# A hybrid decoder layer on one core: three buffers in RWKV's preparation, and small products that wait for the state chain's next step

## Chip, cores and metric

The kernel runs on one core of one Trainium2 chip. The metric is the device time of one execution in microseconds (us); lower is better. Times are medians over runs.

## The reference

One layer (DEPTH 1) on x of shape 1 x 512 x 2048 in float32. The hidden size of the feed-forward part is 5632.

```python
h = rms_norm(x, attn_norm_g)
qa, ka, va, qb, kb, vb, rw = split(h @ w_in)
ya = diff_attention(qa, ka, va, ...)             # 4 heads, two softmaxes subtracted, ALiBi
yb = sliding_window_attention(qb, kb, vb, ...)   # 8 query, 2 key heads, window 128, sinks
feats = token_shift(rw, rwkv_mu)
r, k, v, wl, al, gl = split(feats)               # 16 heads of 64
decay = exp(-exp(-softplus(-(w0 + tanh(wl) @ w2)) - 0.5))
a = sigmoid(a0 + al @ a2);  g = sigmoid(gl) @ g2
kk = normalised(k * k_k);  k = k * (1 + (a - 1) * k_a)
# token by token, for every head:
S = S * w_t + (S @ a_t) b_t^T + v_t k_t^T        # a_t = -kk, b_t = kk * a
y_t = S @ r_t
yc = (group_norm(y) * ln_w + ln_b + bonus) * g
x = x + concat(ya, yb, yc) @ w_out
x = x + (silu(h2 @ w_gate) * (h2 @ w_up)) @ w_down   # h2 = rms_norm(x)
return rms_norm(x, final_norm_g)
```

## The kernel before

**Layout and dense products.** Everything is kept transposed: 128 partitions hold features, 512 columns hold tokens. Each projection onto 128 features is 16 slices of the input's 2048 features, and each slice takes three matmuls, since the float32 operands are split into a high and a low part in a reduced format (high times high, low times high, high times low): 48 "dense" products a projection, which all go through `mm` (L131). A weight is loaded by SyncE's queue (L204), rounded to its high part on ScalarE (ACT, L208) and its low part is taken on VectorE (DVE, L209). The program runs the mixers' 43 projections with a step structure (the last of the gates' inputs, then k, r and v for each of 8 pairs of RWKV heads, then the attention's), then w_out, then the feed-forward part (44 gate, 44 up, then down).

**The small work between them.** The RWKV and attention work is cut into steps, written as Python generators that stand in lanes. After each dense product, `pump` looks at all lanes, and lets each lane whose time is due emit its next step; a generator's `yield` says how much later its next step is due, in a planner's microseconds (`self.now`, which `mm` moves on), or, with nothing, when the planner takes the step's work on DVE and ACT for done. A generator that needs something unfinished yields and looks again at the next pump. TensorE executes in the order in which the products are emitted; the other engines' order is set by a scheduler that heeds priorities. Float32 products of the small steps are not split.

**One pair of RWKV heads** (512 tokens, 8 chunks of 64) goes through these generators:

- `rates` (L457-490): two products z (with w2) and pa (with a2) and from them, on ACT and DVE, the decay W, its inverse V and a.
- `prep` (L494-615): the norm kn, kk, and bk (L526, L531), two operands side by side; the transposes bt of bk in two halves of four, each copied from PSUM to bkn on ACT (L541); ar (L548, L550), holding -kk times W and r times W; zl, copied from ar on ACT (L560); the Gram products gr of bk with ar in two halves u of 4 chunks and 2 heads, in two pieces each with `yield 0.4` between; their parts are masked on DVE (L577) into linv, zl and gr, three masks for each of four PSUM tiles; linv's blocks go to DRAM (L588); then vt (v by token) with its copies to uv (L602), and bon and bv (L607, L612).
- `inverse` (L617-645), lane 1: after the blocks are read back in another layout (x), 31 steps of forward substitution on DVE (xt L637, xy L638), and the store of the result, xi, to DRAM (L642).
- `join` (L648-685), lane 7: `yield 7`, load of xi into linv (L653), `yield 6`, then three groups of 16 products 32x32: px, pt and po, which complete the inverse.
- `chain` (L688-735), lane 2: 8 chunks in order, each with products z, u and S and their copies on ACT and DVE in between, and y into a PSUM tile of its own.
- `post` (L737-765), lane 6: the variance product var, the normalisation, the gate's products g.

bt of pair p waits until the chain of pair p-2 is at its end, since bkn has two buffers; so has every one of ar, zl, gr, uv and linv.

**PSUM** is in pools: pd, two tiles for the dense products; pm, two tiles (z, pa, kn, bt, gr, vt, bon); pc, three (chain, join, post and the attention); py, one for y. A product into a tile waits until the work that read the tile's earlier content is done.

Of the kernel before, what the change touches and what calls it, by code (L numbers as in the profile page):

```python
# [14 lines left out]
P = 128  # L15
# [73 lines left out]
class Kernel:  # L89
    def __init__(self, tc, ins, out, dbg=None, stop=None):  # L90
        self.tc = tc
        self.nc = tc.nc
        self.i = ins
        self.out = out
        self.dbg = dbg or {}
        self.stop = stop
        self.lanes = [[], [], [], [], [], [], [], []]
        self.order = [self.lanes[j] for j in (2, 7, 6, 5, 0, 1, 3, 4)]
        self.done = set()
        self.flags = set()  # L100
        self.now = 0.0
        self.due = {}
        self.free = {"DVE": 0.0, "Activation": 0.0}
        self.last = 0.0
        self.slack = 0.3
        self.lead = 300
# [56 lines left out]
    def pump(self):  # L163
        moved = False
        for lane in self.order:
            if lane:
                name, gen = lane[0]
                if self.due.get(name, 0.0) > self.now:
                    continue
                moved = True  # L170
                self.last = self.now
                try:
                    wait = next(gen)
                    self.due[name] = self.now + wait if wait else self.last + self.slack
                except StopIteration:
                    lane.pop(0)
                    self.done.add(name)
                self.last = self.now
        return moved

    def need(self, name):
        for _ in range(100000):
            if name in self.done:
                return
            if not self.pump():
                self.now = min(self.due[lane[0][0]] for lane in self.order if lane)
# [192 lines left out]
    def mixer_items(self, enter):  # L379
# [35 lines left out]
        self.linv = [lp.tile([P, NCH, P], F32, name=f"linv{j}") for j in range(2)]  # L415
# [3 lines left out]
        keep = rp.tile([P, NCH, 65], F32, tag="pn", name="keep")  # L419
# [37 lines left out]
    def rates(self, hp):  # L457
        nc, rp = self.nc, self.rp
        q = self.in_flight[hp]
        while hp and f"prep{hp - 1}" not in self.done:  # L460
            yield
        if not hp:
            yield 15
        ch = slice(hp * P, (hp + 1) * P)
        w2 = rp.tile([97, P], F32, tag="w2", name=f"w2_{hp}", bufs=4)
        a2 = rp.tile([96, P], F32, tag="w2", name=f"a2_{hp}", bufs=4)
# [27 lines left out]
    def prep(self, hp):  # L494
        nc, rp = self.nc, self.rp
        q = self.in_flight[hp]
        while "k" not in q or f"rates{hp}" not in self.done:
            yield
# [34 lines left out]

        while hp >= 2 and f"loop{hp - 2}" not in self.done:
            yield
        bkn = rp.tile([P, NCH, P], F32, tag="bkn", name=f"bkn{hp}", bufs=2)
        for u in range(2):
            ps = self.pm.tile([P, 4, P], F32, tag="m", name=f"bt{hp}_{u}")
            for n in range(4):
                self.tr(ps[:, n, :], bk[:, u * 4 + n].rearrange("p a c -> p (a c)"))  # L540
            nc.scalar.copy(out=bkn[:, u * 4:u * 4 + 4, :], in_=ps)  # L541
            yield
        q["bkn"] = bkn
        while "r" not in q:
            yield
        r = q["r"]
        ar = rp.tile([P, NCH, 2, C], F32, tag="ar", name=f"ar{hp}", bufs=2)
        nc.vector.scalar_tensor_tensor(out=ar[:, :, 0, :], in0=c3(kk), scalar=-1.0, in1=W[:, :, 0:64],  # L548
                                       op0=ALU.mult, op1=ALU.mult)
        nc.vector.tensor_tensor(out=ar[:, :, 1, :], in0=c3(r), in1=W[:, :, 1:65], op=ALU.mult)  # L550

        nc.vector.tensor_tensor(out=a, in0=a, in1=r, op=ALU.mult)
# [3 lines left out]
        zl = rp.tile([P, 2, NCH, C], F32, tag="zl", name=f"zl{hp}", bufs=2)  # L556
        L = self.linv[hp % 2]
        gr = rp.tile([P, 2, NCH, C], F32, tag="gr", name=f"gr{hp}", bufs=2)
        for h in range(2):
            nc.scalar.copy(out=zl[HALF[h], h, 1:], in_=ar[HALF[h], 1:, 0, :])  # L560
        mask = self.cst("mask", P)
        for u in range(2):
# [3 lines left out]
            for j in range(4):  # L566
                n = 4 * u + j
                for h in range(2):
                    self.mm(ps[h][:, j, :], bk[HALF[h], n], ar[HALF[h], n], start=True, stop=True)
                if j == 1:  # L570
                    yield 0.4
            for h in range(2):
# [7 lines left out]
                masked(zl[ks, h, us], ks, 0)  # L580
                masked(gr[:, h, us], slice(0, P), 1)
        q.update(zl=zl, L=L, gr=gr, ar=ar)
# [8 lines left out]
        while "v" not in q:  # L591
            yield
# [12 lines left out]
        yield  # L605
        rkm = rp.tile([P, P], F32, tag="w2", name=f"rkm{hp}", bufs=4)
# [3 lines left out]
        yield  # L610
# [5 lines left out]
    def inverse(self, q):  # L616
# [7 lines left out]
        y = rp.tile([P, 8, 32], F32, tag="i1", name="xy")  # L624
# [7 lines left out]
        tmp = rp.tile([P, 8, 32], F32, tag="i3", name="xt")  # L632
# [14 lines left out]
    def join(self, q):  # L647
# [3 lines left out]
        yield 7  # L651
        for h, b, bl in blocks:
            nc.sync.dma_start(out=L[bl, :, bl], in_=d[h, b].rearrange("n i g t -> (i g) n t"))  # L653
        yield 6
# [17 lines left out]
        pt = rp.tile([P, NCH, 32], F32, tag="pt", name="pts")  # L672
# [15 lines left out]
    def chain(self, q):  # L688
        nc, rp = self.nc, self.rp
        hp, zl, L, gr, ar, uv, bkn = (q[n] for n in ("hp", "zl", "L", "gr", "ar", "uv", "bkn"))  # L690
        while hp and f"y{hp - 1}" not in self.done:
            yield
        py = self.py.tile([P, T], F32, tag="y", name=f"y{hp}")
        q["g2"] = g2 = rp.tile([P, 2, P], F32, tag="g2", name=f"g2_{hp}", bufs=2)
        nc.sync.dma_start(out=g2, in_=self.i["g2"][:, :, hp * P:(hp + 1) * P])


        for n in range(NCH):
            pz = self.pc.tile([P, C], F32, tag="c", name=f"z{hp}_{n}")
            for h in range(2):  # L700
                ks = slice(0, P) if n else HALF[1 - h]
                self.mm(pz[HALF[h]], zl[ks, h, n], uv[ks, n, h])
# [4 lines left out]
            if n:  # L707
                for h in range(2):
                    self.mm(py[HALF[h], n * C:(n + 1) * C], uv[HALF[h], n, h], ar[HALF[h], n, 1], start=True,
# [12 lines left out]
            if n < NCH - 1:  # L722
# [3 lines left out]
                with self.urgent():  # L726
                    for h in range(2):
# [4 lines left out]
                        else:  # L732
                            nc.vector.tensor_scalar(out=s, in0=pS[hs], scalar1=d, scalar2=None, op0=ALU.mult)
            for h in range(2):
                self.mm(py[HALF[h], n * C:(n + 1) * C], uv[:, n, h], gr[:, h, n], start=(n == 0), stop=True)
            yield
        self.lanes[6].append((f"chain{hp}", self.post(q, py)))  # L737

    def post(self, q, py):
# [10 lines left out]
        yield  # L750
# [4 lines left out]
        yield  # L755
        ps = self.pc.tile([P, T], F32, tag="c", name=f"g{hp}")
        for j in range(2):
            self.mm(ps, q["g2"][:, j, :], self.gl[j], start=(j == 0), stop=(j == 1))
        yield
# [61 lines left out]
    def attention_setup(self):  # L821

        nc = self.nc
        while f"inv{NPAIR - 1}" not in self.done or f"loop{NPAIR - 2}" not in self.done:
            yield
        dist = self.rp.tile([P, 768], F32, tag="ar", name="dist", bufs=2)
# [25 lines left out]
    def diff_head(self, h, q, vtag):  # L852
        nc, rp = self.nc, self.rp
        while "setup" not in self.done:
            yield
        bias = rp.tile([P, T], F32, tag="h", name=f"bias{h}", bufs=2)
        nc.scalar.mul(out=bias, in_=self.dist, mul=DIFF_SLOPES[h])
        while "k" not in q:
            yield
# [3 lines left out]
        def scores(blk):  # L863
# [5 lines left out]
            p = rp.tile([P, 2, T], F32, tag=("bk", "i1")[blk % 2], name=f"pa{h}_{blk}")  # L869
# [16 lines left out]
        def turned(blk):  # L886
# [4 lines left out]
            wt = rp.tile([P, 4, P], F32, tag=("pt", "pn")[blk % 2], name=f"wts{h}_{blk}")  # L891
# [10 lines left out]
        while "v" not in q:  # L902
            yield
        vn = self.natural(q["v"], vtag, f"van{h}")
        while f"chain{NPAIR - 1}" not in self.done:
            yield
# [23 lines left out]
    def swa_values(self, kv):  # L930
        while "v" not in kv:
            yield
# [3 lines left out]
    def swa_tile(self, i, q, kv):  # L936
# [5 lines left out]
        while "q" not in q:  # L942
            yield
# [8 lines left out]
        def scores(n):  # L952
# [5 lines left out]
            p = rp.tile([P, 2, 256], F32, tag=("bk", "i1")[n % 2], name=f"pb{i}_{n}")  # L958
# [19 lines left out]
        def turned(n):  # L978
# [5 lines left out]
            wt = rp.tile([P, 2, 2, P], F32, tag=("pt", "pn")[n % 2], name=f"wtsb{i}_{n}")  # L984
# [28 lines left out]
    def mixes(self, js):  # L1013
# [4 lines left out]
        for n, j in enumerate(js[::2]):  # L1018
            for e in range(2):
                while self.mix[j + e] is None:  # L1020
                    yield
# [269 lines left out]
```

## Time and profile before

| | |
|---|---|
| median of 3 runs | 2465.69 us (2463.95 to 2465.7) |
| the profiled execution | 2460.77 us |
| its span in the profile | 2459.0 us |
| granted TensorE clock, mean | 0.994 |
| ScalarE / VectorE / GpSimd instructions | 1391 / 2121 / 157 |

The profile is of one execution. Its span leaves out 1.8 us of the execution's own time. In a line of groups the columns are: line, engine, operation, output<-inputs, tile shape, count | busy us, mean ns of one | idle us of the engine just before and what ended it. A timeline's row has the start, the duration, and in brackets the idle time ahead of it with its releaser. A window's row has the length of the stretch, then busy time and number of instructions of each engine, then the granted clock (1.00 is full). Matmuls are pipelined, so that a row's duration is longer than its step to the next row's start. PE is TensorE, PEld its weight loads, SPq SyncE's DMA queue.

### The profile page before, as it was taken

The page shows a single profiled execution, that of the slowest core. Times are in us where ns is not written, and L with a number is a line of the kernel's source. Part 1 is how long each engine was busy: PE and PEld are TensorE (multiplying, and loading weights), DVE is VectorE, ACT ScalarE, POOL GpSimd, SP SyncE. Part 2 cuts the span into 40 slices and gives each one's busy share as a digit, 9 for nine tenths or more (in the row PEclk, how much of TensorE's full clock was granted, in tenths as well). Part 3 has the DMA queues.
Part 4 walks back from the last instruction along what each step waited for, and adds up shares of the span by engine and source line. Part 5 has one row for each costly group of instructions (what it writes and reads, how often), then busy time and mean ns, then how long its engine had stood idle before and what let it go on. Part 6 is the DMA issues. An engine that isn't in the chain of part 4 may idle for free.

```text
span 2459.0 us, 30832 instructions
## 1 busy us (share of the span) xinstructions
PE 2415.4 (98%) x12328; PEld 1915.2 (78%) x12328; DVE 1181.9 (48%) x2121; ACT 813.8 (33%) x1391; POOL 99.4 (4%) x157
## 2 busy tenths in 40 slices
PE   8999999999999999999999999999999999999997
PEld 6766666676677778888888888888888888888887
DVE  7567776675544544434343434343434333343437
ACT  5445555444434423322222122222222222222224
POOL 3000000000000003100000000000000000000006
PEclk9999999999999999999999999999999999999999
DMA  5222222222223433222322322322232232232224
GB/s 176 91 77 75 84 75 83 66 82 85 90 86 100 146 124 103 95 95 97 101 95 95 101 96 94 99 98 95 96 101 94 95 101 96 94 100 98 94 96 136
DMA packets 103793, 240.04 MB, mean 98 GB/s; under 512 B 34906, under 2 KB 43746, under 8 KB 103650
## 3 DMA queue, kind: packets, MB, share of 16 engines
q1 hardware_dynamic: 98754, 231.39, 29.4%
q10 hardware_dynamic: 4896, 6.69, 0.8%
q8 instruction: 97, 1.59, 0.3%
q14 instruction: 46, 0.38, 0.0%
HBM read 227.55 MB, written 10.49 MB: 97 GB/s over the span
## 4 chain that ended last, share of the span: by engine, by line
PE 87%; DVE 2%; ACT 1%; DMA 1%; issue 1%; SPq 0%; POOL 0%; DVEq 0%; ACTq 0%; POOLq 0%
PE pg L131 19%; PE pu L131 19%; PE pd L131 19%; PE po L131 7%; PE pd_v L131 3%; PE pd_k L131 2%; PE pd_r L131 2%; PE pd_va L131 2%; PE pd_qa L131 2%; PE pd_qb L131 2%; PE pd_ka L131 1%; PE y L131 1%; PE z L131 1%; PE S L131 1%; PE pd_kb L131 1%
## 5 line engine op out<-in xcount | busy, mean ns | idle before, releaser
L131 PE MATMUL pd<-al,wh_wd 128*128 128x512 f32 (+1 forms) x768 | 285.3, 371 | 0.6 <-DVE al L1141 0.6
L131 PE MATMUL pd<-ah,wh_wd 128*128 128x512 f32 (+1 forms) x768 | 285.5, 372 | 0.4 <-DVE y L1160 0.4
L131 PE MATMUL pd<-ah,wl_wd 128*128 128x512 f32 (+1 forms) x768 | 285.2, 371 | 0.0
L131 PE MATMUL pu<-x1h,wh_wu 128*128 128x512 f32 x704 | 274.3, 390 | 0.0
L131 PE MATMUL pu<-x1l,wh_wu 128*128 128x512 f32 x704 | 273.9, 389 | 0.0
L131 PE MATMUL pu<-x1h,wl_wu 128*128 128x512 f32 x704 | 273.9, 389 | 0.0
L131 PE MATMUL pg<-x1h,wl_wg 128*128 128x512 f32 x704 | 273.9, 389 | 0.0
L131 PE MATMUL pg<-x1l,wh_wg 128*128 128x512 f32 x704 | 273.9, 389 | 0.0
L131 PE MATMUL pg<-x1h,wh_wg 128*128 128x512 f32 x704 | 273.9, 389 | 0.0
L1160 DVE TENSOR_TENSOR y<-y,pd 128x512 f32<-128x512 f32 (+1 forms) x192 | 122.5, 641 | 207.8 <-PE pd L131 207.6
L208 ACT CAST wh_wd<-raw_wd 128x1024 fp32r<-128x1024 f32 x96 | 101.0, 1052 | 356.9 <-PE pd L131 177.2
L208 ACT CAST wh_wu<-raw_wu 128x1024 fp32r<-128x1024 f32 x88 | 92.7, 1053 | 366.7 <-PE pu L131 144.8
L208 ACT CAST wh_wg<-raw_wg 128x1024 fp32r<-128x1024 f32 x88 | 92.7, 1054 | 362.8 <-PE pg L131 144.9
L209 DVE TENSOR_TENSOR wl_wg<-raw_wg,wh_wg 128x1024 fp32r<-128x1024 f32 x88 | 107.8, 1225 | 171.4 <-ACT wh_wg L208 171.4
L209 DVE TENSOR_TENSOR wl_wu<-raw_wu,wh_wu 128x1024 fp32r<-128x1024 f32 x88 | 107.8, 1225 | 133.5 <-ACT wh_wu L208 133.5
L131 PEld LDWEIGHTS pd<-al,wh_wd 128*128 128x128 f32 x768 | 144.7, 188 | 25.7 <-DVE al L1141 0.8
L131 PEld LDWEIGHTS pd<-ah,wh_wd 128*128 128x128 f32 x768 | 144.7, 188 | 25.6 <-issue 0.5
L131 PEld LDWEIGHTS pd<-ah,wl_wd 128*128 128x128 f32 x768 | 144.7, 188 | 24.9
L131 PEld LDWEIGHTS pu<-x1h,wh_wu 128*128 128x128 f32 x704 | 132.1, 188 | 27.6 <-issue 0.2
L131 PEld LDWEIGHTS pu<-x1l,wh_wu 128*128 128x128 f32 x704 | 132.1, 188 | 27.6 <-issue 0.2
L131 PEld LDWEIGHTS pu<-x1h,wl_wu 128*128 128x128 f32 x704 | 132.1, 188 | 27.5
L131 PEld LDWEIGHTS pg<-x1h,wl_wg 128*128 128x128 f32 x704 | 132.1, 188 | 27.4
(357 smaller groups left out, 4100.4 us busy)
## 6 DMA issues: line engine op xcount, KB each, us to landing
raw_wd<-in_w_down SPq DMA_DIRECT2D x96, 512.0 KB, 3.2
raw_wg<-in_w_gate SPq DMA_DIRECT2D x88, 512.0 KB, 3.7
raw_wu<-in_w_up SPq DMA_DIRECT2D x88, 512.0 KB
raw_wo<-in_w_out SPq DMA_DIRECT2D x32, 512.0 KB, 3.5
raw_k<-in_w_in SPq DMA_DIRECT2D x16, 512.0 KB, 3.8
raw_r<-in_w_in SPq DMA_DIRECT2D x16, 512.0 KB, 4.3
raw_v<-in_w_in SPq DMA_DIRECT2D x16, 512.0 KB, 3.7
x<-in_xT SPq DMA_DIRECT2D x16, 256.0 KB, 4.9
```

Of the source, the lines that this page charges most:

```text
L131: self.tc.keep_in_program_order(self.nc.tensor.matmul(out, lhsT, rhs, start=start, stop=stop))
L208: nc.scalar.copy(out=hi[:, :kn * m], in_=s)
L209: nc.vector.tensor_tensor(out=lo[:, :kn * m], in0=s, in1=hi[:, :kn * m].bitcast(F32), op=ALU.subtract)
L1160: nc.vector.tensor_tensor(out=o, in0=o, in1=ps, op=ALU.add)
```

## The change

Four things are edited together.

**Three buffers.** `ar` and `zl` become one tile Z, three blocks of 64 columns for each chunk: blocks 0 and 1 hold, for the two heads, -kk times W in that head's partitions and the masked Gram part in the other's; block 2 holds r times W. The two copies zl<-ar a pair go; -kk times W is written in two operations of 64 partitions in place of one of 128. Z, gr and linv have three buffers each; to make room, w2/a2/rkm share three in place of four, g2 has one, and other tiles move to other tags.

**Riding.** A generator that needs something unfinished yields a condition, kept in `self.until`, and becomes due when the condition holds. Steps with products (all lanes but 1, the substitution and mixes, and 5, the token shifts) are not emitted as soon as they are due, but when the state chain's lane has a step ready, or when one of them has waited longer than `hold` (1.3 of the planner's us while a chain runs, else 0.4). `need` pumps without that rule.

**Order in prep.** The Gram products come first, each half in one step; bt comes after them, both halves in one step, and waits for `keys` of pair p-2 (its chain's last use of bkn) rather than for that chain's end. vt and bon are one step. `chain` waits for its own pair's v; `post` emits g's products together with var's.

**The join** yields 8.0 and 10.0 where it yielded 7 and 6.

The core of the diff:

```diff
+        self.hold = (1.3, 0.4)
+        self.chaining = False
...
+        ready = [lane for lane in self.order
+                 if lane and lane[0][0] not in self.until and self.due[lane[0][0]] <= self.now]
+        ride = not hold or any((self.chaining and lane is self.lanes[2]) or
+                               self.now - self.due[lane[0][0]] > self.hold[not self.chaining]
+                               for lane in ready if not self.alone(lane))
+        for lane in ready:
+            if not ride and not self.alone(lane):
+                continue
...
-        self.linv = [lp.tile([P, NCH, P], F32, name=f"linv{j}") for j in range(2)]
+        self.linv = [lp.tile([P, NCH, P], F32, name=f"linv{j}") for j in range(3)]
...
-        while hp >= 2 and f"loop{hp - 2}" not in self.done:
-            yield
-        bkn = rp.tile([P, NCH, P], F32, tag="bkn", name=f"bkn{hp}", bufs=2)
-        for u in range(2):
-            ps = self.pm.tile([P, 4, P], F32, tag="m", name=f"bt{hp}_{u}")
...
-            yield
-        q["bkn"] = bkn
...
+        Z = rp.tile([P, NCH, 3, C], F32, tag="Z", name=f"Z{hp}", bufs=3)
+        for h in range(2):
+            s = HALF[h]
+            nc.vector.scalar_tensor_tensor(out=Z[s, :, h, :], in0=c3(kk)[s], scalar=-1.0, in1=W[s, :, 0:64],
+                                           op0=ALU.mult, op1=ALU.mult)
+        nc.vector.tensor_tensor(out=Z[:, :, 2, :], in0=c3(r), in1=W[:, :, 1:65], op=ALU.mult)
...
-            nc.scalar.copy(out=zl[HALF[h], h, 1:], in_=ar[HALF[h], 1:, 0, :])
...
-                    self.mm(ps[h][:, j, :], bk[HALF[h], n], ar[HALF[h], n], start=True, stop=True)
-                if j == 1:
-                    yield 0.4
+                    self.mm(ps[h][:, j, :], bk[HALF[h], n], Z[HALF[h], n, h::2 - h], start=True, stop=True)
...
+        if hp >= 2 and f"keys{hp - 2}" not in self.done:
+            yield lambda: f"keys{hp - 2}" in self.done
+        bkn = rp.tile([P, NCH, P], F32, tag="bkn", name=f"bkn{hp}", bufs=2)
+        for u in range(2):
+            ps = self.pm.tile([P, 4, P], F32, tag="m", name=f"bt{hp}_{u}")
+            for n in range(4):
+                self.tr(ps[:, n, :], bk[:, u * 4 + n].rearrange("p a c -> p (a c)"))
+            nc.scalar.copy(out=bkn[:, u * 4:u * 4 + 4, :], in_=ps)
+        yield
...
-        yield 7
+        yield 8.0
...
-        yield 6
+        yield 10.0
```

Three places in the order of TensorE's products show what the edits move. In the names, bt7_0 is a tile of pair 7, half 0, gr7_1_0 one of pair 7's Gram tiles of half 1, S4_6 and z4_7 products of pair 4's chain for chunks 6 and 7, and a last number only counts tiles; pd_ is a dense product.

The first place, on TensorE: the join of pair 5 (px, 16 products). Before, it stands between the two pieces of a Gram half of pair 6:

```order
L131 MATMUL gr6_0_0_4492<-ar6_4464,bk6_4212 128x128 [waits Activation_49]
L131 MATMUL gr6_0_1_4493<-ar6_4464,bk6_4212 128x128 [waits Activation_49]
...
L131 MATMUL pd_r7_4407<-xh12_204,wl_r7_8_4241 128x512
L131 MATMUL px_4499<-cc_76,linv1_482 32x32 [waits DMAHW3_49]
L131 MATMUL px_4499<-cc_76,linv1_482 32x32 [waits DMAHW5_49]
L131 MATMUL px_4499<-cc_76,linv1_482 32x32 x14
L131 MATMUL gr6_0_0_4492<-ar6_4464,bk6_4212 128x128
L131 MATMUL gr6_0_1_4493<-ar6_4464,bk6_4212 128x128
```

After the change, the same join on TensorE:

```order
L134 MATMUL u4_6_4441<-zs4_6_4403,linv1_482 128x64 [waits Activation_49]
...
L134 MATMUL pd_r7_4422<-xh2_116,wl_r7_0_4210 128x512
L134 MATMUL S4_6_4450<-uv4_3183,bkn4_3133 64x64 [waits Activation_49] x2
L134 MATMUL y4_4128<-gr4_2948,uv4_3183 64x64 x2
L134 MATMUL px_4457<-cc_76,linv2_483 32x32 [waits DMAHW3_49,PE_49]
L134 MATMUL px_4457<-cc_76,linv2_483 32x32 [waits DMAHW6_49]
L134 MATMUL px_4457<-cc_76,linv2_483 32x32 x14
L134 MATMUL pd_r7_4422<-xh3_126,wh_r7_0_4209 128x512
```

It now follows a step of the state chain without a dense product between, among the dense products of projection r of pair 7 as before.

The second place, on TensorE: the transposes bt of pair 7. Before, they come ahead of the pair's Gram products, and in two steps:

```order
L135 MATMUL bt7_0_5034<-cc_76,bk7_4895 128x128 [waits DVE_49]
L135 MATMUL bt7_0_5034<-cc_76,bk7_4895 128x128 x3
...
L131 MATMUL var5_5051<-ysq5_5028,cc_76 128x512 [waits Activation_49]
L135 MATMUL bt7_1_5055<-cc_76,bk7_4895 128x128 x4
...
L131 MATMUL gr7_1_0_5141<-ar7_5081,bk7_4895 128x128 [waits DVE_49,PE_49]
L131 MATMUL gr7_1_1_5142<-ar7_5081,bk7_4895 128x128 [waits DVE_49,PE_49]
```

After the change:

```order
L134 MATMUL gr7_1_0_5012<-Z7_4885,bk7_4796 128x128
L134 MATMUL gr7_1_1_5013<-Z7_4885,bk7_4796 128x128
L138 MATMUL bt7_0_5034<-cc_76,bk7_4796 128x128 [waits DVE_49,PE_49]
L138 MATMUL bt7_0_5034<-cc_76,bk7_4796 128x128 x3
L138 MATMUL bt7_1_5040<-cc_76,bk7_4796 128x128 [waits Activation_49]
L138 MATMUL bt7_1_5040<-cc_76,bk7_4796 128x128 x3
L134 MATMUL pd_qa0_4919<-xh10_188,wh_qa0_8_4730 128x512
```

Both halves come right behind the last Gram products, the first waiting for DVE and the second for ACT.

The third place, on TensorE: the rates of pair 5, z5 and pa5. Before:

```order
L131 MATMUL bon4_3374<-a4_2751,rkm4_3372 128x512 [waits DVE_49]
L131 MATMUL pd_r5_3184<-xl14_225,wh_r5_8_3015 128x512
L131 MATMUL S3_0_3377<-uv3_2673,bkn3_2468 64x64 [waits Activation_49] x2
L131 MATMUL y3_3355<-gr3_2523,uv3_2673 64x64 x2
L131 MATMUL z5_3393<-wl_453,w2_5_3389 128x512 [waits DMAHW1_49,PE_49]
L131 MATMUL pa5_3397<-al_463,a2_5_3390 128x512 [waits DMAHW2_49,DVE_49]
```

After the change:

```order
L134 MATMUL bon4_3195<-a4_2637,rkm4_3193 128x512 [waits PE_49]
L134 MATMUL pd_k5_3041<-xl12_205,wh_k5_8_2852 128x512
L134 MATMUL var2_3200<-ysq2_3177,cc_76 128x512 [waits Activation_49]
L134 MATMUL g2_3204<-sgl0_475,g2_2_2787 128x512 [waits DMAHW0_49]
L134 MATMUL g2_3204<-sgl1_569,g2_2_2787 128x512
L134 MATMUL z5_3216<-wl_453,w2_5_3212 128x512 [waits DMAHW6_49,PE_49,Activation_49]
L134 MATMUL pa5_3220<-al_463,a2_5_3213 128x512 [waits DMAHW7_49,Activation_49]
```

pa waited for DVE (bv of pair 4) and now waits for ACT (the read of z's PSUM tile).

More of the change, by code (lines that the diff above doesn't have):

```diff
@@ L184, in need @@
                 return
-            if not self.pump():
-                self.now = min(self.due[lane[0][0]] for lane in self.order if lane)
+            if not self.pump(False):
+                self.now = min(self.due[lane[0][0]] for lane in self.order if lane and lane[0][0] not in self.until)
         raise AssertionError(name)
@@ L496, in prep @@
         q = self.in_flight[hp]
-        while "k" not in q or f"rates{hp}" not in self.done:
-            yield
+        if "k" not in q or f"rates{hp}" not in self.done:
+            yield lambda: not ("k" not in q or f"rates{hp}" not in self.done)
         W, V, a = q["W"], q["V"], q["a"]
@@ L590, in prep @@
         self.lanes[1].append((f"sub{hp}", self.inverse(q)))
-        while "v" not in q:
-            yield
+        if hp >= 2 and f"keys{hp - 2}" not in self.done:
[7 more added lines that the diff above has]
+        yield
+        q["bkn"] = bkn
+        if hp >= 2 and f"loop{hp - 2}" not in self.done:
+            yield lambda: f"loop{hp - 2}" in self.done
+        if "v" not in q:
+            yield lambda: not ("v" not in q)
         v = q["v"]
@@ L749, in post @@
         nc.scalar.activation(sq, sq, AF.Exp, scale=-0.5)
-        yield
+        ps = self.pc.tile([P, T], F32, tag="c", name=f"g{hp}")
+        for j in range(2):
+            self.mm(ps, q["g2"][:, j, :], self.gl[j], start=(j == 0), stop=(j == 1))
         nc.vector.tensor_tensor(out=sq, in0=py, in1=sq, op=ALU.mult)
@@ L901, in diff_head @@
         scores(1)
-        while "v" not in q:
-            yield
+        if "v" not in q:
+            yield lambda: not ("v" not in q)
         vn = self.natural(q["v"], vtag, f"van{h}")
-        while f"chain{NPAIR - 1}" not in self.done:
-            yield
+        if f"chain{NPAIR - 1}" not in self.done:
+            yield lambda: not (f"chain{NPAIR - 1}" not in self.done)
         yield
@@ L930, in swa_values @@
     def swa_values(self, kv):
-        while "v" not in kv:
-            yield
+        if "v" not in kv:
+            yield lambda: not ("v" not in kv)
         kv["vn"] = self.natural(kv["v"], "W", "vbn")
```

142 lines of the change are left out of this document (70 added, 72 removed).

## The prediction

> **What bounds the kernel now.** The page comes first. The PE row gives the share of TensorE, and the chain that ended last says what the end hangs on.
>
> ```profile
> PE 2415.4 (98%) x12328; PEld 1915.2 (78%) x12328; DVE 1181.9 (48%) x2121; ACT 813.8 (33%) x1391; POOL 99.4 (4%) x157
> PE 87%; DVE 2%; ACT 1%; DMA 1%; issue 1%; SPq 0%; POOL 0%; DVEq 0%; ACTq 0%; POOLq 0%
> ```
>
> TensorE (PE) is busy 98% of the span and carries 87% of the chain. The change alters no dense product, so it can only give back time in which PE stands still, runs at a lower clock, or pays for switching between kinds of products. Those are some 44 us of idle (2459.0 less 2415.4) and whatever the clock costs inside the busy time. I therefore read the PE groups with shapes kept apart, for the idle time ahead of each group:
>
> ```profile
> L131 PE MATMUL px<-cc,linv 32*32 32x32 f32 x256 | 7.6, 204 | 9.8 <-DMA linv<-xi 9.7
> L135 PE MATMUL bt<-cc,bk 128*128 128x128 f32 x64 | 9.6, 273 | 2.3 <-DVE bk L531 2.3
> L131 PE MATMUL pd_k<-xh,wl_k 128*128 128x512 f32 x128 | 52.4, 409 | 2.2 <-DVE wl_k L209 2.2
> L131 PE MATMUL pa<-al,a 96*128 96x512 f32 x16 | 8.3, 598 | 0.5 <-DVE bv L612 0.5
> L135 PE MATMUL wt<-cc,pa 128*128 128x128 f32 x40 | 7.2, 279 | 4.3 <-DVE pa L881 2.8 <-DVE st L874 1.5
> L131 PE MATMUL sa<-ka,qa 64*128 64x128 f32 x16 | 2.0, 322 | 0.6 <-DVE ka L782 0.6
> L135 PE MATMUL p_van<-cc,va 128*128 128x128 f32 x16 | 2.6, 286 | 0.6 <-DVE va L782 0.6
> ```
>
> The largest is px, the first product of `join`, which waits for the inverse to come back from DRAM. The timeline of pair 5 shows one such wait: the substitution's last step, the store of xi, the load into linv, and the product.
>
> ```profile
> 461.47 0.17 DVE L638 TENSOR_TENSOR xy<-xy,xt 128x8 f32<-128x8 f32 x1
> ...
> 461.81 2.52 SPq L642 DMA_DIRECT2D xi<-xy  x4
> ...
> 465.95 1.85 SPq L653 DMA_DIRECT2D linv<-xi  x4
> ...
> 467.93 0.31 PE L131 MATMUL px<-cc,linv 32*32 32x32 f32 x2 [2.78 <-DMA linv<-xi]
> ...
> 468.78 1.06 PE L131 MATMUL px<-cc,linv 32*32 32x32 f32 x30 [0.55 <-DMA linv<-xi]
> ```
>
> From the last step's end (461.64) to the point where px runs freely (468.78) are 7.1 us. PE stood there 2.78 + 0.55 = 3.3 us too early. What follows the wait is worse than the wait. The windows, cut at the edges where the granted clock changes, are these (columns: PE, PEld, DVE, ACT, POOL busy, clock, DMA share, GB/s):
>
> ```profile
> 156.60:163.40 6.80, 6.16 (x62) 4.25 (x64) 1.27 (x3) 0.72 (x2) 0.10 (x1) 0.50 0.33 90
> 467.20:477.40 10.20, 8.93 (x106) 6.56 (x107) 3.38 (x8) 2.71 (x6) 0.00 (x0) 0.50 0.08 13
> 583.30:586.70 3.40, 3.40 (x11) 2.02 (x10) 0.00 (x0) 2.35 (x5) 0.00 (x0) 0.50 0.79 265
> ```
>
> Three stretches at half clock, 6.80, 10.20 and 3.40 us long, each one starting in or just behind a px wait. At half clock, half of the PE-busy time is lost: (6.16 + 8.93 + 3.40) / 2 = 9.2 us. To see what trips the clock I asked for PE alone in the 3.4 us ahead of the last two, and in another stretch with little work:
>
> ```profile
> 136.10:139.50 3.40, 1.81 (x9) 1.00 0.00 0
> 463.80:467.20 3.40, 1.35 (x11) 1.00 0.77 208
> 579.90:583.30 3.40, 0.92 (x33) 1.00 0.86 244
> ```
>
> Idle 3.40 - 1.81 = 1.6 us was not followed by half clock; idle of 2.05 and 2.5 was. The limit lies between 1.6 and 2.05 us of idle in 3.4 us.
>
> **The change part by part.** The profiled execution took 2460.77 us, 4.9 us under the median of 2465.69. I make the sum against 2460.77 and carry the difference over to the median.
>
> *The join later.* `yield 7` becomes 8.0 and `yield 6` 10.0, 5 us more in the planner's count of products, and as these products now ride with the state chain, they come later still. PE was at most 3.3 us early, so I take the whole wait as gone: 9.7 us (bounds 0 and 9.7), and with it the half clock, 9.2. What hides the DMA round trip then is dense products of the next projection, which need nothing from it. Behind the later join wait the chain's steps; a third linv, gr and a/r buffer lets the next pair's Gram products go ahead without them.
>
> *bt moved behind the Gram products.* The old wait of bt for bk (2.3) goes, since bk is long written when bt comes. But where pair 7's two bt halves stood apart before, with dense products and var between them, the Gram half gr7_1 is now followed at once by both (the second place in the order, above). The first transpose waits for a PSUM buffer of gr7_1, so for its masks on DVE; the second half waits for the ACT copy of the first. The same stands in pairs 0, 1 and 3; in 2, 4, 5 and 6 bt comes dozens of products later. What masks and copy cost, the timelines of before show:
>
> ```profile
> 150.29 0.71 PE L131 MATMUL gr<-ar,bk 64*128 64x128 f32 x8
> ...
> 151.03 0.42 DVE L577 TENSOR_TENSOR linv<-gr,cc 64x256 f32<-64x256 f32 x1 [0.36 <-PE gr L131]
> ...
> 151.46 0.43 DVE L577 TENSOR_TENSOR zl<-gr,cc 64x256 f32<-64x256 f32 x1
> ...
> 151.91 0.42 DVE L577 TENSOR_TENSOR gr<-gr,cc 128x256 f32<-128x256 f32 x1
> ```
>
> ```profile
> L541 ACT COPY bkn<-bt 128x512 f32<-128x512 f32 x16 | 9.3, 582 | 4.8 <-PE bt L135 4.7
> ```
>
> From the products' end (151.00) to the third mask's end (152.33) are 1.3 us, with a little for the release 1.5; the copy takes 0.58, and with its start and release 0.9. So 2.4 us a pair in four pairs: 9.6 us. The lower bound is 1.3 + 0.6 = 1.9 a pair (7.6); the upper adds a weight subtraction that may stand ahead of the masks (1.23, estimated from wl_v's in the same trace's timeline below), so 3.6 a pair (14.5).
>
> ```profile
> 460.13 1.23 DVE L209 TENSOR_TENSOR wl_v<-raw_v,wh_v 128x1024 fp32r<-128x1024 f32 x1
> ```
>
> Does this trip the clock? Each place has 2.4 us idle within some 2.8. The clock's stretches are 3.4 us long; by the limit above, 2.05 of the 2.4 must fall into one. The 2.8 us may lie in it whole (3.4 - 2.8 = 0.6 us of starts), or slip out by 0.35 at either end, so about 1.2 / 3.4, one in three. One stretch at half clock costs 1.7, so 4 x 1/3 x 1.7 = 2.3 us (bounds 0 and 6.8). [...] This trace halved the clock behind a gap of 2.37:
>
> ```profile
> 582.27 1.04 PE L131 MATMUL px<-cc,linv 32*32 32x32 f32 x32 [2.37 <-DMA linv<-xi]
> ```
>
> so I keep the 2.3.
>
> *The rates.* In the third place of the order pa no longer waits for DVE's bv but for ACT, which must read z out of the PSUM buffer first. Before, in pair 2:
>
> ```profile
> 171.64 1.13 PE L131 MATMUL z<-wl,w 97*128 97x512 f32 x2
> ...
> 172.60 1.02 PE L131 MATMUL pa<-al,a 96*128 96x512 f32 x2
> ...
> 172.80 0.60 ACT L375 ACTIVATE sg<-z 128x512 f32<-128x512 f32 x1
> ```
>
> There pa starts at 172.60; if it must wait for the read's end (173.40) it loses 0.8, with the release 0.85. In the order of after this holds for pairs 3, 5, 6 and 7: 3.4 us; the old 0.5 for bv goes. z of pairs 1 and 2 now waits a little for the uv copies of vt: 0.4 together (an estimate from 0.367 a copy, below). Both of these are too short to trip the clock.
>
> ```profile
> L602 ACT COPY uv<-vt 64x256 f32<-64x256 f32 x32 | 11.7, 367 | 4.7 <-PE vt L131 4.2
> ```
>
> *Riding.* PE's order has 344 runs of small products between dense ones before and 297 now, 47 fewer, with the same products in them. What a run's edge costs:
>
> ```profile
> 93.19 0.48 PE L131 MATMUL pd_v<-xh,wl_v 128*128 128x512 f32 x1
> 93.50 0.39 PE L131 MATMUL pd_v<-xh,wh_v 128*128 128x512 f32 x1
> 93.73 0.40 PE L131 MATMUL pd_v<-xl,wh_v 128*128 128x512 f32 x1
> ```
>
> The first dense product behind a run takes 0.31 us to the next, the others 0.23: 0.08 x 47 = 3.8 us (0 if the runs' own switches take it back; twice that if the run's front costs as much). Longer runs also queue more on ACT ahead of the chain's copies, which the chain's first steps after the rates then wait for: 0.7, an estimate of two copies' length.
>
> *The rest.* PE's wait for wl_k at pair 2 (2.2) should go, as the Gram and bt products ahead of it shift PE's arrival; bounds 0 and 2.2. The attention's steps are now taken two dense products later, which covers the waits of sa and p_van (0.6 + 0.6) and, I take it, a quarter of wt's 4.3 (1.1): 2.3, bounds 0 and 5.5. The merged tile Z drops 16 ACT copies and adds one 64-row pass on DVE per pair:
>
> ```profile
> L560 ACT COPY zl<-ar 64x448 f32<-64x448 f32 x16 | 9.0, 564 | 2.4 <-DVE ar L548 2.2
> L548 DVE SCALAR_TENSOR_TENSOR ar<-kk,W 128x512 f32<-128x512 f32 x8 | 5.5, 686 | 0.3
> ```
>
> 9.0 us less on ACT (33% busy), 5.5 more on DVE (48%): no wait of PE is for either, so 0, while dense products cover them. SP's loads of w2, a2 and g2 out of fewer buffers sit behind steps that finished a pair earlier: 0.
>
> **The sum.** Removed: 9.7 + 9.2 + 2.3 + 2.2 + 0.5 + 2.3 + 3.8 = 30.0. Added: 9.6 + 2.3 + 3.4 + 0.4 + 0.7 = 16.4. Net -13.6: 2447.2 for a profiled execution, 2452 for the median.
>
> **The rivals.** *More is gained:* the clock never halves at bt (2.3), all of the attention's waits go (3.2 more) and a run's edge costs double (3.8 more): 2452 - 9 = 2443. For it speaks that every half-clock stretch of before followed one unbroken wait of 2.37 us or more, and bt's is in two parts; against it, that three things must all fall well.
>
> *Riding gives nothing and bt trips the clock each time:* the edges' 3.8 gone and 6.8 instead of 2.3 at bt: 2452 + 3.8 + 4.5 = 2460.3. For it speaks that wider runs contain the same switches, and that DVE, with the substitution running beside, may mask late. [...]
>
> *Slower: px still waits.* The substitution's 31 steps run on DVE between prep's masks and the weight subtractions. Since Gram products of the next pair may now come earlier by the third buffer, their masks (0.42 each, 12 a pair, 5 us) and the extra Z pass (0.7) can fall inside the substitution; if its end slips by more than the 5 us that the join was put back, PE is early again: 9.7 + 9.2 stay and with bt at its worst 4.5 more, so 2452 + 18.9 + 4.5 = 2475. It decides from a slip of some 5 us; the share of 48% on DVE speaks against it, px waits of 3.3 where it was already crowded for it.
>
> *The change doesn't do what it says* (riding too rare to matter) is within the second rival's 3.8.
>
> **How the numbers follow.** What can be told from no change is about 0.2%, 4.9 us: 2460.8 to 2470.6. Forecast (2447 to 2458, the bounds of bt, wl_k and the edges) 0.52; more gained 0.14; the second rival 0.18, half of it on each side of 2460.8; slower 0.10; mixes between forecast and no change 0.06, in the same band. So faster 0.52 + 0.14 + 0.09 + 0.01 = 0.76, same 0.14, slower 0.10. The range reaches from the larger gain, 2443, past the second rival, to 2466, inside the band of no change; left out are the slower case (0.10) and the far tails of the others.
>
> **What would show it.** Right: px groups without an idle row for linv<-xi; no half-clock stretch at px; bt with 9 to 10 us of idle for the DVE masks and the ACT copy together, in four pairs; pa with some 3.4 us for ACT sg. Wrong: px still idle by several us (the slower rival), bt idle above 14 or clock stretches at all four bt places (the second), or PE's busy time unchanged although half clock is gone, which would mean that the 9.2 was not lost to the clock.

## The result, and the profile after

| | before | after |
|---|---|---|
| median | 2465.69 us (4 runs, 2463.95 to 2466.34) | 2439.93 us (4 runs, 2437.91 to 2443.1) |
| ratio | | 0.9898, 95% interval 0.9881 to 0.9915 |
| the profiled execution, its span | 2460.77, 2459.0 | 2443.1, 2441.3 |
| its mean granted clock | 0.994 | 0.996 |

The change made the kernel 25.8 us faster; the forecast was 13.7 (2452), with 2443 as the range's low end. Two differences have to be explained, not one: the profiled executions lie 17.7 us apart, the medians 25.8.

The page's first line and the groups of PE that answer to those of before:

```profile
PE 2403.6 (98%) x12328; PEld 1912.5 (78%) x12328; DVE 1185.9 (49%) x2129; ACT 808.4 (33%) x1375; POOL 99.7 (4%) x158
```

```profile
L134 PE MATMUL px<-cc,linv 32*32 32x32 f32 x256 | 5.5, 192 | 0.0
L138 PE MATMUL bt<-cc,bk 128*128 128x128 f32 x64 | 10.5, 302 | 8.9 <-DVE gr L586 6.2 <-ACT bkn L608 2.7
L134 PE MATMUL pd_k<-xh,wl_k 128*128 128x512 f32 x128 | 54.2, 423 | 0.0
L134 PE MATMUL pa<-al,a 96*128 96x512 f32 x16 | 8.6, 618 | 2.7 <-ACT sg L397 2.7
L138 PE MATMUL wt<-cc,pa 128*128 128x128 f32 x40 | 7.2, 278 | 1.7 <-DVE pa L905 1.7
L134 PE MATMUL sa<-ka,qa 64*128 64x128 f32 x16 | 2.0, 322 | 0.1
L138 PE MATMUL p_van<-cc,va 128*128 128x128 f32 x16 | 2.6, 286 | 0.1
L134 PE MATMUL gr<-Z,bk 64*128 64x128 f32 x256 | 19.0, 285 | 0.9 <-DVE gr L586 0.9
```

px waits for nothing (9.8 before), the wait for wl_k is gone (2.2), the attention's waits shrank. bt took over: 8.9 us, for the masks and for the copy of its own first half, and pa waits 2.7 for ACT. At pair 7's bt the timeline shows the two waits as they were foreseen, 1.49 and 0.68 us:

```profile
505.49 0.42 DVE L586 TENSOR_TENSOR linv<-gr,cc 64x256 f32<-64x256 f32 x1 [0.33 <-PE gr L134]
505.94 0.43 DVE L586 TENSOR_TENSOR Z<-gr,cc 64x256 f32<-64x256 f32 x1
...
506.38 0.42 DVE L586 TENSOR_TENSOR gr<-gr,cc 128x256 f32<-128x256 f32 x1
...
506.95 0.63 PE L138 MATMUL bt<-cc,bk 128*128 128x128 f32 x4 [1.49 <-DVE gr L586]
...
507.61 0.58 ACT L608 COPY bkn<-bt 128x512 f32<-128x512 f32 x1 [2.66 <-PE bt L138]
...
508.25 0.66 PE L138 MATMUL bt<-cc,bk 128*128 128x128 f32 x4 [0.68 <-ACT bkn L608]
```

And what follows a bt wait is what followed px before. The half-clock stretches of the changed kernel (columns as in the prediction's windows), each behind a bt:

```profile
150.60:157.43 6.83, 6.15 (x19) 4.79 (x19) 0.93 (x3) 1.50 (x3) 0.73 (x5) 0.50 0.47 95
270.07:273.48 3.41, 3.41 (x9) 1.77 (x8) 0.00 (x0) 1.19 (x2) 0.00 (x0) 0.50 0.33 51
509.00:512.42 3.42, 3.42 (x6) 1.35 (x5) 0.09 (x1) 1.84 (x3) 0.00 (x0) 0.50 0.64 131
```

(6.15 + 3.41 + 3.42) / 2 = 6.5 us, against 9.2 before (9.3 in the table, where the edges aren't rounded). The half is an estimate from the granted 0.50. In before's last such stretch (from 583.27) dense products start 0.43 us apart, 1.9 times the 0.2268 that they take on average in the feed-forward part:

```profile
585.40 0.63 PE L131 MATMUL pd_ka<-xh,wh_ka 128*128 128x512 f32 x1
585.83 0.63 PE L131 MATMUL pd_ka<-xl,wh_ka 128*128 128x512 f32 x1
586.26 0.59 PE L131 MATMUL pd_ka<-xh,wl_ka 128*128 128x512 f32 x1
```

Between the first product of pair 0's k projection and the first of the feed-forward part, the two traces differ like this. "Idle" sums PE's waits over 0.06 us; "clock" is half of the time not idle in half-clock stretches; "the rest" is what remains of the time when these two and 0.2268 us for each of the 2784 dense products are taken off, so the small products, their switches and shorter waits.

| us | before | after | difference | forecast |
|---|---|---|---|---|
| idle | 21.2 | 14.8 | -6.4 | -2.9 |
| clock | 9.3 | 6.5 | -2.8 | -6.9 |
| the rest | 280.2 | 272.3 | -7.9 | -3.8 |
| sum of the three | | | -17.1 | -13.6 |

0.6 more was gained ahead of that point. From here to 25.8 are 8.1 us that no comparison of these two profiles can show.

### The profile page after: what moved, and what is told of

Same layout as the page of the kernel before. It is cut to its first block, busy times and chain, and to the rows that moved or that the text cites. A ratio compares the mean times of both kernels' runs of the same rounds, so it can differ in the third digit from the quotient of the medians.

```text
span 2441.3 us, 30869 instructions
## 1 busy us (share of the span) xinstructions
PE 2403.6 (98%) x12328; PEld 1912.5 (78%) x12328; DVE 1185.9 (49%) x2129; ACT 808.4 (33%) x1375; POOL 99.7 (4%) x158
## 4 chain that ended last, share of the span: by engine, by line
PE 71%; DVE 1%; POOL 0%; issue 0%; ACT 0%; DVEq 0%; ACTq 0%; POOLq 0%
PE pg L134 20%; PE pu L134 20%; PE pd L134 19%; PE po L134 7%; PE pd_qb L134 2%; PE pd_va L134 1%; PE sb L134 0%; PE pd_ka L134 0%; PE ob L134 0%; PE pd_qa L134 0%; POOL acc L1130 0%; PE wtb L138 0%; DVE y L1228 0%; PE oa L134 0%; PE sa L134 0%
## 5 line engine op out<-in xcount | busy, mean ns | idle before, releaser
L134 PEld LDWEIGHTS pg<-x1l,wh_wg 128*128 128x128 f32 x704 | 132.1, 188 | 27.4
```

Source lines behind the costliest of these rows:

```text
L134: self.tc.keep_in_program_order(self.nc.tensor.matmul(out, lhsT, rhs, start=start, stop=stop))
```

## The experiments

Each was timed with runs of the kernel before on the same chip in between; ratios are against those.

**The join's two numbers alone.** The kernel before with

```diff
-        yield 7
+        yield 8.0
...
-        yield 6
+        yield 10.0
```

> The kernel before with the join's two numbers alone changed (7 and 6 to 8.0 and 10.0). If the gain of the change comes from px coming late enough, 9.7 us of waits and the half clock behind them go and the time falls by 15 to 20 us, to about 2448. The rival: with two buffers a later join only makes the state chain late; the chain's steps then come close together and wait on ACT and DVE, some 20 us in the order of this kernel, and the time is 2460 to 2475.

2461.44 us, ratio 0.9977 (0.9967 to 0.9987): 5.5 faster, at the low end of the rival's range. PE's groups in this kernel:

```profile
L131 PE MATMUL px<-cc,linv 32*32 32x32 f32 x256 | 6.6, 198 | 5.6 <-DMA linv<-xi 5.4
L131 PE MATMUL S<-uv,bkn 128*64 128x64 f32 x224 | 20.5, 249 | 1.5 <-ACT uv L720 1.5
L131 PE MATMUL u<-zs,linv 128*128 128x64 f32 x128 | 22.6, 259 | 1.2 <-ACT zs L705 1.2
```

px still waits 5.6 us, in two of eight pairs, and the chain's steps wait longer (S 0.9 and u 0.0 before). The two numbers don't remove the wait.

**The numbers taken back.** The changed kernel with 7.0 and 6.0.

> The changed kernel with the join's two numbers back at 7 and 6. In the trace of the changed kernel px stands 13 to 22 us behind the substitution's last step, and needs about 7; if so, 5 us less still leaves no px wait, and the time is within 5 us of the changed kernel's 2439.9. If the two numbers carry the gain, px waits come back with their half clock: 2455.

2442.74 us, ratio 0.9896 (0.9883 to 0.9909) against 0.9898 of the change: no difference that can be told. px idles 0.0 here too. In the trace of before px stands 6 to 12 us behind the store of xi, in that of the change 13 to 34, in this one 7 to 45. So px came late enough without the join's numbers, which my first term rested on, though in one pair (7.3 us) with nothing to spare.

**No riding.** The changed kernel with

```diff
-        self.hold = (1.3, 0.4)
+        self.hold = (-1.0, -1.0)
```

> The changed kernel with every step emitted as soon as it is due (hold below zero), so that nothing rides. PE's order then has 22 more runs of small products (325 against 303). By the prediction's edge of 0.08 us that is 1.8 us, with the attention's waits (2.5 us of gaps) 4 in all: 2444. If an edge costs 0.17 us, as the difference of the two traces suggests, and the attention's waits return: 2447 to 2450. If riding carries most of the gain: over 2455.

2451.4 us, ratio 0.9929 (0.9917 to 0.9941). 11.5 slower than with riding (10.2 when each is taken against the runs of before on its own chip), more than any case with small edges allowed, less than most of the gain. The expectations count runs in another way than the prediction (303 for the changed kernel, where it has 297), so only differences within one count are used. px waits 0.0 without riding as well, so px does not need riding to come late; it stands 22 to 53 us behind the store of xi here. The 15.5 us to before belong to the buffers, the join's numbers, the order in prep and the merged steps together. PE's groups show what came back, z's wait for uv's copies and the attention's:

```profile
L134 PE MATMUL z<-wl,w 97*128 97x512 f32 x16 | 8.6, 618 | 2.6 <-ACT uv L624 2.6
L138 PE MATMUL wt<-cc,pa 128*128 128x128 f32 x40 | 7.1, 276 | 4.1 <-DVE pa L905 2.6 <-DVE st L898 1.5
```

**bt in steps of its own.** The changed kernel with a bare yield ahead of bt and between its halves, so that PE does dense products while the masks and the copy run:

```diff
+        yield
         bkn = rp.tile([P, NCH, P], F32, tag="bkn", name=f"bkn{hp}", bufs=2)
...
             nc.scalar.copy(out=bkn[:, u * 4:u * 4 + 4, :], in_=ps)
-        yield
+            yield
```

> The changed kernel with a bare yield ahead of bt and between bt's two halves, so that neither follows at once what it waits for. The trace of the changed kernel shows 8.9 us of idle at bt and three of its four places followed by half clock (13.7 us, so 5 to 6 us lost). If that is right and the clock's share holds in most executions: 8.9 + 4 less, 14 more runs cost 1.1 to 2.4: about 2429. If the clock rarely trips there: 2433. If the waits move to other products instead: 2438 to 2442.

2428.83 us, ratio 0.984 (0.9828 to 0.9853), as the first case said. It beats both kernels: 11 us under the change. The bt group:

```profile
L138 PE MATMUL bt<-cc,bk 128*128 128x128 f32 x64 | 9.7, 274 | 0.0
```

The waits at bt are gone, and the mean clock of its four executions is 0.997 to 0.998. The added waits of the forecast (9.6 at bt) were therefore real and avoidable. px waits 0.8 us again in one pair.

**Before, once more.** The same program, for another profile.

> The program of before once more, for another of its profiles. Fifteen of its executions show granted clocks of 0.989 to 0.992 where the profile that the prediction read shows 0.994, and 2.15 us more time for each 0.001 less. If the half clock behind the px waits was under-read in that one profile, this one, at a clock of 0.991 to 0.992, has 10 to 15 us more of half-clock stretches in the mixers than the 20.5 of the first, at px or at other waits of the same kernel, and the same idle time within 2 us. If the stretches are the same and the time still differs, the difference lies elsewhere.

2466.95 us, ratio 0.9999 (0.9989 to 1.0009). Its profiled execution has a span of 2468.4 us at a clock of 0.990, where the one that the prediction read has 2459.0 at 0.994. Idle at px is 10.0 and at bt 2.3 (9.8 and 2.3 there):

```profile
L131 PE MATMUL px<-cc,linv 32*32 32x32 f32 x256 | 7.6, 205 | 10.0 <-DMA linv<-xi 9.9
L135 PE MATMUL bt<-cc,bk 128*128 128x128 f32 x64 | 10.6, 291 | 2.3 <-DVE bk L531 2.3
```

Its half-clock stretches, in the same columns as above:

```profile
93.88:97.29 3.41, 3.41 (x12) 2.72 (x11) 0.00 (x0) 0.59 (x1) 0.00 (x0) 0.50 0.08 30
141.66:145.08 3.42, 3.42 (x11) 2.75 (x12) 3.42 (x9) 2.11 (x4) 0.00 (x0) 0.50 0.58 169
158.73:175.80 17.07, 15.47 (x140) 11.33 (x141) 3.07 (x7) 3.73 (x11) 0.11 (x2) 0.50 0.31 78
476.17:483.00 6.83, 6.83 (x66) 5.06 (x58) 2.44 (x6) 1.73 (x5) 0.00 (x0) 0.50 0.01 2
588.81:599.05 10.24, 10.19 (x112) 6.59 (x112) 0.56 (x1) 5.55 (x13) 0.00 (x0) 0.50 0.32 101
```

41.0 us in place of 20.5, so (3.41 + 3.42 + 15.47 + 6.83 + 10.19) / 2 = 19.7 us lost in place of 9.2. Two waits that kept the full clock in the first profile, at bt (93.88) and for wl_k (141.66), are followed by half clock here, and the stretches behind px are longer. The 10.5 more cover the 9.4 by which the spans differ. There are 20 us more of such stretches, where 10 to 15 were expected, and the execution's clock is lower than the 0.991 to 0.992 assumed.

**Two buffers in effect.** The changed kernel, with a pair's Z held back until the chain of two pairs before ends:

```diff
+        if hp >= 2 and f"loop{hp - 2}" not in self.done:
+            yield lambda: f"loop{hp - 2}" in self.done
         Z = rp.tile([P, NCH, 3, C], F32, tag="Z", name=f"Z{hp}", bufs=3)
```

> The changed kernel, but a pair's a/r tile, and with it its Gram products, waits until the chain of two pairs before is at its end, as two buffers would make it. If the third buffer only keeps the order free and the gain is from riding and the join, the time stays within 5 us of 2439.9. If the third buffer is what lets riding work, the chain's steps pile up behind the late inverse: the order of this kernel then has some 60 us of short waits for ACT and DVE (an upper bound, since they follow one another), and the time is 2455 to 2490.

2483.03 us, ratio 1.0062 (1.0048 to 1.0076): slower than before, 43 us over the change. PE's groups with the longest idle time:

```profile
L138 PE MATMUL bt<-cc,bk 128*128 128x128 f32 x64 | 14.0, 358 | 16.5 <-DVE gr L588 11.1 <-ACT bkn L610 5.4
L134 PE MATMUL gr<-Z,bk 64*128 64x128 f32 x256 | 22.8, 306 | 5.2 <-DVE gr L588 4.6 <-DVE xt L659 0.5
L134 PE MATMUL S<-uv,bkn 128*64 128x64 f32 x224 | 22.0, 253 | 4.3 <-ACT uv L744 4.3
```

Gram products, bt and chain steps now stand together and wait for each other's DVE and ACT work, at a clock of 0.985. Counted as in the table above, idle is 17.3 us more than in the change and half clock costs 22.0 more. The rest of the change, as it stands, needs the third buffer. px idles 0.0 here too. What this kernel, the one without riding and the one with the numbers back have in common with the change, and not with before, is the order in prep with its merged steps, the one tile Z, and conditions in place of looking again at each pump.

**Both holds doubled**, on the kernel with bt in steps of its own (2.6 and 0.8 for 1.3 and 0.4).

> As the kernel with bt in steps of its own (2428.8), with both holds doubled, 2.6 and 0.8: 303 runs of small products in place of 317. By 0.08 us a run 1.1 us less, by 0.15 2.1 less: 2427 to 2428. The rival: what waits longer comes too late for those who need it (z and pa of the rates, the last attention steps ahead of w_out, where this order shows up to 3 us of waits), which costs more than the edges: 2430 to 2436.

2449.23 us, ratio 0.9922 (0.9909 to 0.9936), 20 over the kernel it was made from, and worse than the rival case. Fewer runs took 2.7 us off "the rest" (268.3 in place of 271.0), but idle rose from 6.2 to 20.5 and what half clock costs from 1.7 to 11.1. PE's groups show the waits:

```profile
L134 PE MATMUL px<-cc,linv 32*32 32x32 f32 x256 | 6.9, 203 | 8.8 <-DMA linv<-xi 8.8
L138 PE MATMUL wtb<-cc,pb 128*128 128x128 f32 x56 | 9.3, 284 | 5.9 <-DVE pb L999 5.9
L134 PE MATMUL po<-mh,wh_wo 128*128 128x512 f32 x256 | 102.5, 401 | 2.4 <-ACT mh L1061 2.4
```

px stood 6 to 7 us behind the store of xi again in three pairs and waited in two of them, and the last attention steps came too late for w_out.

**Riding taken apart**, again on the kernel with bt in steps of its own: none (holds -1 and -1), only while a chain runs (1.3 and -1), only while none runs (-1 and 0.4).

> As the kernel with bt in steps of its own (2428.8), without riding: 335 runs in place of 317, and the attention's waits back. Riding was worth 11.5 us in the changed kernel. If that was edges (0.08 to 0.15 a run, 2 to 3 here) and attention waits (4): 2435. If it was mostly half clock that happened to follow bt there, riding is worth little here: 2430 to 2433. If riding is worth as much as there: 2440.

> As the kernel with bt in steps of its own (2428.8 with riding, 2438.3 without), riding only while a state chain runs: 318 runs of small products, as with riding, but the attention's waits and those of the rates as without (11 us against 6 of idle in the order's places). If the runs carry riding's 9.4 us: 2430. If waits carry it (the feed-forward test gave only 0.04 us for an edge, so 0.7 for 18 of them): 2436 to 2438.

> The other half: riding only while no chain runs, 335 runs as without riding, but the attention's steps two dense products later, so that their waits go. If the runs carry riding's 9.4 us: 2437. If the waits carry it: 2429 to 2432.

| riding | runs | time, us | ratio | idle | clock | the rest |
|---|---|---|---|---|---|---|
| always | 317 | 2428.83 | 0.984 (0.9828 to 0.9853) | 6.2 | 1.7 | 271.0 |
| never | 335 | 2438.27 | 0.9882 (0.9868 to 0.9895) | 13.0 | 0.0 | 275.8 |
| in chains | 318 | 2439.49 | 0.9896 (0.9879 to 0.9913) | 15.5 | 1.5 | 273.5 |
| outside chains | 335 | 2434.88 | 0.9874 (0.9857 to 0.9891) | 8.6 | 3.4 | 274.2 |

The last three columns are of one profiled execution each, counted as in the table further up. Without riding the time lies between the case of edges and waits (2435) and that of riding's full worth (2440). Riding in chains alone saves the runs and gains nothing, a little over the case in which the waits carry it: "the rest" falls by 2.3 and idle rises by 2.5. Riding outside them saves no run, takes the attention's waits, and lies between its two cases. PE's groups without riding:

```profile
L138 PE MATMUL wt<-cc,pa 128*128 128x128 f32 x40 | 7.1, 276 | 4.3 <-DVE st L903 2.0 <-DVE st L899 1.5 <-DVE pa L906 0.7
L138 PE MATMUL p_van<-cc,va 128*128 128x128 f32 x16 | 2.6, 287 | 1.1 <-DVE va L805 1.1
```

The same groups with riding outside the chains only:

```profile
L138 PE MATMUL wt<-cc,pa 128*128 128x128 f32 x40 | 7.1, 276 | 1.4 <-DVE pa L906 1.3
L138 PE MATMUL p_van<-cc,va 128*128 128x128 f32 x16 | 2.6, 286 | 0.2
```

The four do not add: each order lets some other product wait for its operand (in chains only, wt waits 6.7 us; outside them only, z waits 2.7 at one place). In the profiles riding is worth 6.8 us of idle and 4.8 of the rest here, against 1.7 of clock; in the medians 9.4.

**The edge of a run, by itself.** 344 spare products 128x64 in the feed-forward stage, whose result is not used, one by one or four together:

```diff
         for k in range(len(wts[0])):
             self.dense_k(ps, wts, rhs, k, len(wts[0]), m, cols)
+            if extra and k in (2, 5, 8, 11):
+                for _ in range(1):
+                    self.mm(self.spare[:, 0:64], self.cst("ident", P), self.cst("ident", P)[:, 0:64])
```

> The kernel with bt in steps of its own, with 344 spare float32 products 128x64 added to the feed-forward stage (their result is not used), each one alone between dense products: 344 more runs. The measure is the feed-forward stage, which waits for nothing, against that of the next kernel.

> The same 344 spare products, four together: 86 more runs, 258 fewer than the kernel with them apart. If a run's edge costs 0.08 us, as the prediction took it, this stage is 21 us shorter than there; at 0.15 to 0.17, as the traces of before, after and the kernels without riding suggest, 39 to 44 us; under 10 us if the products' own switches take it back, and then riding's gain is all waits and clock.

One execution each: 2522.84 and 2511.75 us, both at a clock of 0.997. The feed-forward stage, from its first product to the end, takes 1550.6 and 1540.7 us in the two profiles. That is the case under 10 us, by little. 9.9 / 258 = 0.038 us for an edge, half of the 0.08 that I took from a row. A product in a group is not free of a switch either. In the timelines a lone product (which the rows count x2) stands 0.14 us ahead of the next dense product, four together 0.81, so 0.20 each:

```profile
1200.85 0.33 PE L134 MATMUL spare<-cc 128*128 128x64 f32 x2
1200.99 0.47 PE L134 MATMUL pu<-x1h,wh_wu 128*128 128x512 f32 x1
```

```profile
1207.16 1.00 PE L134 MATMUL spare<-cc 128*128 128x64 f32 x8
1207.97 0.48 PE L134 MATMUL pg<-x1h,wh_wg 128*128 128x512 f32 x1
```

## Why the prediction came out too high

**The clock: the first step that failed.** "I make the sum against 2460.77 and carry the difference over to the median", with a half-clock term of 9.2 read from that one execution. The prediction saw that the profile was 4.9 us under the median and did not ask what the 4.9 were. They were clock, as far as later executions tell: 15 of before have mean clocks of 0.989 to 0.993 against the profile's 0.994, and each 0.001 less goes with 2.15 us more (1.5 and 2.1 in two further sets of 15 and 9). One of these, at 0.994, took 2460.63 us, as long as the profile's. The second profile of before shows where, 19.7 us lost behind the same waits. The changed kernel's profile errs to the other side: 2443.1 at 0.996 is the longest of its four executions, two others have 0.998 and 2438. So 4.9 + 3.2 = 8.1 us of the gain are no part of a difference of the two profiles, just what was missing. With them the clock gave 2.8 + 8.1 = 10.9 where 6.9 was forecast.

The clock is not the whole miss. The forecast fell 12.2 us short of the gain (25.8 against 13.6): the clock has 4.0 of it, "the rest" 4.1, idle 3.5, and 0.6 lie ahead of the stretch that the table counts. The idle's part is made of small pieces, mostly 1.3 at the attention, 1.3 at bt and pa, and 1.6 at the chain, where the 0.7 set down for ACT's longer queue did not come and the 0.9 by which S waited before went; gr takes back 0.9.

That the same idle costs 9 us in one execution and 20 in another goes with where the stretches start. In before they last 6.827, 10.240 and 3.413 us; the second and third start 310.613 and 426.666 us behind the first (467.216 and 583.269 behind 156.603), 91.0 and 125.0 times 3.413. In its second profile the later ones start 14.0, 19.0, 112.0 and 145.0 such steps behind the first, in the change 35.0 and 105.0. So in these three profiles the granted clock went to half on a grid, whose place differs from execution to execution, and with it whether a wait of 2 us falls into one window or is shared by two. PE in four windows of the change that end on its grid, with bt in them:

```profile
102.82:106.23 3.41, 1.98 (x12) 1.00 0.71 190
147.19:150.60 3.41, 1.26 (x15) 1.00 0.26 77
266.66:270.07 3.41, 1.24 (x13) 1.00 0.77 194
505.59:509.00 3.41, 1.38 (x10) 1.00 0.56 133
```

The first, 1.98 us busy, was followed by full clock, the others by half. bt's two waits are alike in the first, third and fourth, 1.49 and 0.68 us; of the first one's, 0.7 us lie ahead of the window. I had put one bt place in three; it was three in four here, one in four in the kernel with the join's numbers back, three in three without riding, three in seven with two buffers in effect. For the medians, the prediction's clock terms, -9.2 and +2.3, should have been some -14.1 (9.2 + 4.9) and +3.3 (6.5 - 3.2).

**px.** Gone, as forecast, but not by "the join later": with the numbers back it stayed gone, with the numbers alone it did not go. That the term had the right size is luck. (PE was 2.95 + 0.57 = 3.5 us early at pair 0, not "at most 3.3".) Neither riding nor the third buffer is needed either, since px idled 0.0 without each, though two parts were never taken out at once. With the join's new numbers and no riding, px stands 7 to 16 us behind the store of xi in the order of before, and 22 to 53 in that of the change. This points to the order in prep with its merged steps, which was not tried alone, so that it is argued and not shown.

**bt and pa.** 9.6 and 3.4 forecast, 8.9 and 2.7 measured; the places (pairs 0, 1, 3 and 7) were right, and so were the two causes. The remedy experiment gave them back, with the clock.

**Riding: the second step that failed.** The term of 3.8 for 47 edges was right in sign and too small: "the rest" fell by 7.9. The two traces show where. From each product's start to the next one's, with waits and half clock taken off, the dense products of the stretch take 705.0 us before and 695.7 after, the small products 206.3 and 208.0. A dense product just ahead of a run takes 0.29 us on average and one just behind it 0.35, the others 0.23, in both kernels. That is 0.18 a run, where the prediction took 0.08 from one row behind a run and left the front to its upper bound; 47 runs of 0.18 are 8.5. In the test with the spare products an edge is 0.04, since the group takes part of it back, and the dense product ahead of a run takes 0.23 there. So the 0.06 at the front of the real runs may be waits too short to be counted, which stays open.

Among the small products, the Gram products in one step instead of two gained: from 24.8 us of busy time, in the row of before below, to the 19.0 above, the time at half clock included; by their steps to the next product's start, with the half clock taken off, 20.9 to 18.2, so 2.7.

```profile
L131 PE MATMUL gr<-ar,bk 64*128 64x128 f32 x256 | 24.8, 312 | 0.0
```

bt, g and the others took 4.4 more. Riding as a whole was worth 10.2 to 11.5 us in the changed kernel. In the two-by-two test it gave 6.8 us of waits and 4.8 of "the rest"; how much of the latter the saved runs carry is not settled, since riding outside the chains saves none and took 1.6 off it.

**Attention.** 2.3 forecast; wt, sa and p_van went from 5.5 to 1.9, so 3.6.

**The rivals.** The larger gain (2443) was the nearest. Of its three conditions one came true, the edge at double its price; the attention's waits went in part, and the clock did halve at bt; the clock that the medians had to gain it did not name. The second rival's "riding gives nothing" is refuted by the kernel without riding. The slower rival's px wait did not come (0.0). What two buffers do (2483) is another mechanism, waits of bt, the Gram products and the chain, with px idle 0.0.

## What to carry to other kernels

Before a half-clock term is taken from a profile, compare that execution's granted clock with those of the timed executions; where they differ, the same idle can have another price there (9.2 us at 0.994, 19.7 at 0.990, in before). When a product is moved up to what it depends on, look for the copy or mask between: dense products put back between them were worth 11 us here. Batching small work came with some 0.15 to 0.2 us less for each run saved in these traces, and cost far more where it made an operand late (20 us with both holds doubled), so count the waits in the order before and after, and not the batches alone.

## What was not expected of the hardware

In these runs no one busy time parts the windows that kept the clock from those that lost it. Of 3.41 us, 1.65 busy was followed by half clock in the kernel with bt in steps of its own, and 1.70 in the one that rides outside the chains only. 1.68 was not in the kernel with the join's numbers back, nor 1.54 in the one with the join's numbers alone. All four, 1.71 to 1.87 us idle, lie within the 1.6 to 2.05 between which the prediction read a limit. PE in these windows, in this order:

```profile
145.37:148.78 3.41, 1.65 (x9) 1.00 0.39 143
```

```profile
9.10:12.51 3.41, 1.70 (x6) 1.00 0.85 298
```

```profile
384.20:387.61 3.41, 1.68 (x20) 1.00 0.38 111
```

```profile
88.00:91.41 3.41, 1.54 (x7) 1.00 0.00 0
```

Nor does the sum of idle time set what half clock costs: in the tables above 14.8 us of idle came with 6.5 in the change, 15.5 with 1.5 in the kernel that rides in chains only. What else counts in it stays open.
